# Spreading the indirect gathers of a retrieval layer evenly between the steps of the main work

## The chip, the cores and the metric

The kernel runs on one core of one Trainium2 chip. The metric is device time in microseconds (us) for one execution of the whole program. Lower is better.

## The reference, cut to what matters

One inference step of a one-layer encoder for 1024 prompt rows and 128 sample rows, D = 1024. A mixer (gated convolution, RWKV-7 recurrence, output projection) comes first. A product-key retrieval over 16384 single-neuron experts follows, and it is what the change touches:

```python
sc, pos = lax.top_k(cand, 16)                 # per token and head: the 16 best experts, 8 heads
eidx = jnp.take_along_axis(cidx, pos, axis=-1)
gate = jax.nn.softmax(sc, axis=-1)
u = jnp.take(U, eidx, axis=0)                 # 128 rows of 1024 for every token
act = jax.nn.gelu(jnp.einsum('thkd,td->thk', u, xt))
out = jnp.einsum('thk,thkd->td', gate * act, jnp.take(V, eidx, axis=0))
```

## The kernel before

The 1152 rows are nine tiles ("rows" in the code) of 128 tokens. `base(g)` runs the mixer and the scores for three groups of three tiles: a long middle part (input projections, recurrence), then the merge with `w_pab`, the output projection with `w_o`, and 16 blocks of `peer_wq` with top-16 selections on VectorE. `route` turns the selections of a tile into expert indices and gates.

The retrieval is done in two ways. Four tiles (`DENSE` = 3, 4, 5, 6) go through the whole expert table in `dense()`: a gates stage first, then 128 blocks of experts, each with 24 matmuls of 512 columns in `hidden` and its share of `out_half`, which has 48 such matmuls for half an output of four blocks. The other five tiles gather. A tile needs 128 indirect DMAs from `peer_u`, each of 128 rows of 1024 floats (512 KB), each used by one VectorE multiply with a sum (`dot` in `sparse_u`), and then 128 from `peer_v`, used in groups of four by 8 matmuls that add into PSUM (`summed` in `sparse_v`). These are the u gathers and the v gathers; all go through the queue of GpSimd (POOL) and share the seven buffers `gt` (`NGT`).

`run(main)` places the gathers. The main work is a Python generator, and at each of its `yield`s `run` looks at `P.ns`, a count of the matmul time written so far (162 ns for a float32r matmul of 384 columns, 216 ns for one of 512, and 216 ns for a float32 one of 128). While the side's clock `state[1]` is behind `P.ns`, one more gather is written and the clock goes on by `pace`: outside the dense stage 900 ns where a v tile and a u tile run together, 1500 ns where one runs alone; in the dense stage, what is left of it divided by the gathers left. `split_w` (called for each block of weights) sets a clock that is behind to `P.ns`. `quiet` stops the gathers while `middle` runs its 15 serial steps of inverse on VectorE; what was held up follows at the next `yield` in one go. `side()` takes from the generators in the order 0 0 0 0 0 1 1 1 0 1, where 0 is v and 1 is u, and `sparse_v` has yields that count for no step. The result is: four v gathers, three u gathers, the `summed` of these four v, one u gather. A `dot` is written behind the next u gather; a `summed` comes two gathers after its last row where v is alone.

What is written is not yet the order on an engine. The program is built with a scheduler that goes by its own model of times: an instruction written earlier has precedence, but one that isn't ready there (its buffer not free, its data not landed) is passed by later ones. `behind` ties a `dot` or a `summed` behind the last main instruction of the moment at which it is written. Outside the dense stage, the main matmuls are chained in their written order. On the chip each engine then takes its instructions in the order so fixed.

Of the kernel before, what the change touches and what calls it, by code (L numbers as in the profile page):

```python
# [31 lines left out]
NSL = 25  # L32
LAT = 350
SPREAD = (16, 8)
PACE_B = (900, 1500)
EARLY = 40e3
NGT, NGD = 7, 0
AWAY = [4, 5, 6, 7]
WDMA = 0
QUIET = True  # L40
# [56 lines left out]
def body(ctx, tc, A):  # L97
# [73 lines left out]
                              reason="order of emission")  # L171

    mains = [None, None]
    state = [None, 0.0]
    quiet = [False]

    def mm_ps(shape=(128, 512)):
# [139 lines left out]
    def base(g):  # L317
# [498 lines left out]
        for d in range(KB):  # L816
            if gts[d] is None:
                yield from gates(d)
            back(d)
            if d >= 2:  # L820
                back(d + 1)
            gt = gts[d]
            w = split_w(A["w_pab"][d])
            for q, (yh, yl) in enumerate(((ya_h, ya_l), (yb_h, yb_l))):
                ps = mm_ps()
                proj(ps[:, :n], w, ((lambda k: yh[k]), (lambda k: yl[k])), n, [(4 * q + k, k) for k in range(4)])
                V.scalar_tensor_tensor(gt[q][:, :n], gt[q][:, :n], 1.0, ps[:, :n], op0=OP.add, op1=OP.mult)
            V.tensor_tensor(gt[0][:, :n], gt[0][:, :n], gt[1][:, :n], op=OP.add)
            ms.append(gt[0])
            yield  # L830
# [7 lines left out]
        for hf in range(2):  # L838
            pss = [mm_ps() for _ in tiles]
            for kp in range(4):  # L840
                for kk_, (a, b_) in enumerate(split_w(A["w_o"][hf, kp])):
                    k_ = 2 * kp + kk_
                    mh, ml = split_x(ms[k_][:, :n], "sl", [128, n], NSL)
                    for j, ps in enumerate(pss):
                        ts = slice(j * 128, (j + 1) * 128)
                        P.matmul(ps, mh[:, ts], a, start=k_ == 0, stop=False)
                        P.matmul(ps, mh[:, ts], b_, start=False, stop=False)
                        P.matmul(ps, ml[:, ts], a, start=False, stop=k_ == KB - 1)
                yield
            for j, ps in enumerate(pss):  # L850
                V.tensor_tensor(x2s[j][:, hf * 512:(hf + 1) * 512], ps, x2s[j][:, hf * 512:(hf + 1) * 512], op=OP.add)
        for j, x2 in enumerate(x2s):
# [35 lines left out]
        for hp in range(16):  # L888
            if hp == 8 and not last:
                rows[g + 1] = rows_of(g + 1)  # L890
            ps = mm_ps()
            w = split_w(A["peer_wq"][hp])
            for i, _ in enumerate(proj_steps(ps[:, :n], w, ((lambda k: qh[:, k, :n]), (lambda k: ql[:, k, :n])), n,
                                             full)):
                if i == 3 and hp:
                    top(hp - 1, q)
            q = slot()
            S.activation(q[:, :n], ps[:, :n], AF.Copy)
            yield
# [101 lines left out]
        yield 6 if row == 0 else 2 * SPREAD[until[0] is not None]  # L1001

    more = [None, 0]
    both = [False]

    def gathered():

# [6 lines left out]
    def sparse_u(row, ei, et, gate):  # L1014
        xn = T(sp, [128, D], F32, "xn", 1)
        nc.sync.dma_start(xn, xn2_d[row])
        n2bc = T(sp, [128, D], F32, "gt", NGT)
        nc.sync.dma_start(n2bc, A["norm2_g"].partition_broadcast(128))
        V.tensor_tensor(xn, xn, n2bc, op=OP.mult)
        hu = T(sp, [128, 128], F32, "hu", 3)  # L1020

        def dot(k, ug):
            behind(V.scalar_tensor_tensor(ug, ug, 1.0, xn, op0=OP.mult, op1=OP.mult, accum_out=hu[:, k:k + 1]),
                   mains[0])

        due = None
        for k in range(128):
            ug = gathered()
            G.indirect_dma_start(out=ug, out_offset=None, in_=A["peer_u"],  # L1029
                                 in_offset=bass.IndirectOffsetOnAxis(ap=ei[:, k:k + 1], axis=0))  # L1030
            if due:
                dot(*due)
            due = k, ug
            yield True
        dot(*due)
        sparse_v_q.append((row, hu, et, gate))

    def sparse_v(row, hu, et, gate):
        S.activation(hu, hu, AF.Gelu_apprx_tanh)
        V.tensor_tensor(hu, hu, gate.rearrange("p h k -> p (h k)"), op=OP.mult)  # L1040
        pv = T(psv, [128, D], F32, "sv", 1)
        P.transpose(pv[:, 0:128], hu, ident, side=True)
        ct_ = T(sp, [128, 128], F32, "hu", 3)
        V.tensor_copy(ct_, pv[:, 0:128])

        cw = cex[:, :1024].rearrange("p (two c t w) -> p two c t w", two=2, c=4, w=32)
        c4 = ct_.rearrange("p (c b t) -> p c b t", c=4, t=4)

        def fill(n):
            if n < 8:  # L1050
                V.tensor_copy(cw[:, n % 2, :, :, 31], c4[:, :, n])

        def summed(i, vgs):

            prev = mains[1]
            for hf in range(2):
                for c in (3, 2, 1, 0):
                    lo = 32 * (16 * (i // 4 % 2) + 4 * c + i % 4) + 31 - i
                    q = 32 * c
                    mm = P.matmul(pv[q:q + 32, hf * 512:(hf + 1) * 512], cex[:, lo:lo + 32],  # L1060
                                  vgs[c][:, hf * 512:(hf + 1) * 512], start=i == 0, stop=i == 31, side=True)
                    behind(mm, prev)
                    prev = mm
            if i % 4 == 0:
                fill(i // 4 + 1)

        fill(0)
        due = None
        for i in range(32):
            vgs = []  # L1070
            for c in range(4):
                if c == 2 and due:
                    summed(*due)
                    due = None
                t = 32 * c + i
                vg = gathered()
                G.indirect_dma_start(out=vg, out_offset=None, in_=A["peer_v"],  # L1077
                                     in_offset=bass.IndirectOffsetOnAxis(ap=et[:, t:t + 1], axis=0))
                vgs.append(vg)
                yield True  # L1080
            due = i, vgs
            yield False
            if both[0]:
                summed(*due)
                due = None
                yield False
        if due:
            summed(*due)
        live[0] -= 1
        y = T(sp, [128, D], F32, "gt", NGT)  # L1090
        nc.sync.dma_start(y, x2_d[row])
        for hf in range(2):
            V.tensor_tensor(y[:, hf * 512:(hf + 1) * 512], pv[:, hf * 512:(hf + 1) * 512],
                            y[:, hf * 512:(hf + 1) * 512], op=OP.add)
        finish(row, y, pv)
# [9 lines left out]
    def dense():  # L1105
# [92 lines left out]
        def out_half(eg, hf, ps_):  # L1198
            po = [T(pd, [128, 512], F32, "po", 4) for _ in range(nd)]
            for c in range(EG):  # L1200
# [8 lines left out]
                for j in range(nd):  # L1209
                    ts = slice(j * 128, j * 128 + 128)  # L1210
                    P.matmul(po[j], ph[:, ts], h, start=c == 0, stop=False)
                    P.matmul(po[j], ph[:, ts], lo, start=False, stop=False)
                    P.matmul(po[j], pl[:, ts], h, start=False, stop=c == EG - 1)
            for j in range(nd):
                V.tensor_tensor(acc[:, j, hf * 512:(hf + 1) * 512], po[j], acc[:, j, hf * 512:(hf + 1) * 512],
                                op=OP.add)

        def produced(k):
            g = T(dp, [128, ND], F32, "ge", HLEAD + 2)
            if k in ahead:  # L1220
                nc.sync.dma_start(g, g_d[ahead.index(k)])
            else:
                for _ in hidden(k, g):
                    pass
            return g

        def loaded(eg):
# [1 line left out]
            nc.sync.dma_start(cc, c_d[:, :, :, EG * eg:EG * eg + EG, :].rearrange("j g p a t -> p (j g) a t"))  # L1229
            return cc  # L1230

        gs = [produced(k) for k in range(HLEAD)]
        ccs = [loaded(0)]
        prev = None
        for eg in range(128 // EG):
            cc = ccs.pop(0)
            cur = []
            for c in range(EG):
                k = eg * EG + c
                if k + HLEAD < 128:  # L1240
                    gs.append(produced(k + HLEAD))
                if c == 1 and eg + 1 < 128 // EG:
                    ccs.append(loaded(eg + 1))
                g = gs.pop(0)
# [5 lines left out]
                V.tensor_tensor(pl, g, f32(ph), op=OP.subtract)  # L1250
                cur.append((ph, pl))
                if prev is not None and c % 2 == 1:
                    out_half(eg - 1, c // 2, prev)
                yield
            prev = cur
        for hf in range(2):
            out_half(128 // EG - 1, hf, prev)
            yield
        for j, row in enumerate(DENSE):
            finish(row, acc[:, j])  # L1260
            yield
# [2 lines left out]
    def side():  # L1264

        while True:
# [2 lines left out]
            if two == [None, None]:  # L1269
                return  # L1270
            while two[0] or two[1]:
                for i in (0, 0, 0, 0, 0, 1, 1, 1, 0, 1):
                    both[0] = two[1] is not None
                    if two[i] is None:
                        continue
                    got = next(two[i], None)
                    if got is None:
                        two[i] = None
                    elif got:
                        steps[0] += 1  # L1280
                        yield two.count(None)


# [8 lines left out]
    def run(main):  # L1292

        for _ in main:
            mains[:] = V.last, P.last
            while state[1] < P.ns and not quiet[0]:
                if state[0] is None:
                    if not (sparse_q or sparse_v_q):
                        state[1] = P.ns
# [4 lines left out]
                    state[0] = None  # L1304
                else:
                    state[1] += pace(kind)

    def routes():
        while rest:
# [105 lines left out]
```

## Time and profile before

| | |
|---|---|
| time, median of 3 runs | 3957.97 us (3956.65 to 3962.18) |
| the profiled execution | 3941.97 us, span 3940.2 us |
| mean granted TensorE clock | 0.932 of full speed |
| gathers | 640 of each kind, 671.55 MB of 1065.24 MB moved |

The profile is of one execution. A busy share says how much of a stretch an engine worked; PEclk is the granted TensorE clock, 1.00 being 2.4 GHz and 0.50 being 1.2 GHz. A wait names the engine that stood idle, the tile that it was to write, and what ended the wait.

### The profile page before, as it was taken

The numbers are of one execution on the slowest core, as the hardware profiler recorded it, in microseconds if no ns is written. First come the engines' busy times: TensorE is split into PE (matmuls) and PEld (weight loads), VectorE is DVE, ScalarE is ACT, GpSimd is POOL, SyncE is SP. The second block draws the span as 40 slices with busy tenths as digits, with TensorE's granted clock in tenths as the row PEclk, the third lists the DMA queues.
The fourth block names the chain that finished last, engine by engine and source line by source line (L and its number), as shares of the span: only waits on it lengthen the run. The fifth ranks groups of instructions, "written<-read, shape, count | busy, mean of one in ns | idle before, by whom it ended". The sixth has DMA issues, their size and how long they took to land. (4 is left out here: it accounts for less than half of the span.)

```text
span 3940.2 us, 56486 instructions
## 1 busy us (share of the span) xinstructions
PE 3416.1 (87%) x18870; PEld 2633.5 (67%) x18870; DVE 2769.8 (70%) x7554; ACT 1486.2 (38%) x3511; POOL 1644.5 (42%) x1553
## 2 busy tenths in 40 slices
PE   7999977878877786887767999699999999999998
PEld 6778876656665564555555777477777777776676
DVE  4655799887788777758688865499976666664344
ACT  5454533344332332332325877522232222232222
POOL 1000004444455565555555555455544444443331
PEclk9999988878988897888888999899999999999999
DMA  3212527666898888788998989999999989998884
GB/s 101 76 59 88 167 87 258 207 200 196 309 340 302 312 296 300 275 299 309 336 322 296 333 323 337 344 329 362 338 333 330 327 311 330 322 318 294 296 291 161
DMA packets 434019, 1065.24 MB, mean 270 GB/s; under 512 B 47040, under 2 KB 127040, under 8 KB 431680
## 3 DMA queue, kind: packets, MB, share of 16 engines
q0 software_dynamic: 184464, 671.55, 48.0%
q1 hardware_dynamic: 201312, 271.04, 20.8%
q10 hardware_dynamic: 47952, 119.03, 8.2%
q8 instruction: 150, 2.46, 0.2%
q14 instruction: 141, 1.16, 0.1%
HBM read 1000.55 MB, written 61.28 MB: 269 GB/s over the span
## 5 line engine op out<-in xcount | busy, mean ns | idle before, releaser
L1029 POOL DMA_INDIRECT gt<-peer_u,ei x640 | 764.5, 1194 | 1160.4 <-DVE gt L159 442.5
L159 DVE SCALAR_TENSOR_TENSOR gt<-gt,xn 128x1024 f32<-128x1024 f32 x640 | 770.2, 1220 | 230.6 <-DMA gt<-peer_u,ei 212.5
L1077 POOL DMA_INDIRECT gt<-peer_v,et x640 | 713.3, 1115 | 484.1 <-PE sv L142 283.4
L142 PE MATMUL mm<-xT,wh 128*128 128x384 f32 (+1 forms) x2880 | 891.7, 368 | 21.4 <-ACT wh L246 21.2
L142 PE MATMUL po<-vh,ph 128*128 128x512 f32 x2048 | 651.7, 392 | 8.1 <-ACT vh L1205 7.8
L142 PEld LDWEIGHTS mm<-xT,wh 128*128 128x128 f32 x2880 | 561.7, 200 | 88.3 <-issue 41.4
L142 PE MATMUL mm<-xT,wl 128*128 128x384 f32 (+1 forms) x1440 | 513.6, 357 | 57.5 <-DVE wl L159 56.0
L142 PE MATMUL sv<-gt,c 128*32 128x512 f32 x2560 | 338.1, 650 | 146.4 <-DMA gt<-peer_v,et 142.2
L142 PEld LDWEIGHTS po<-vh,ph 128*128 128x128 f32 x2048 | 385.0, 188 | 105.3 <-ACT vh L1205 10.3
L142 PE MATMUL ph<-xth,uh 128*128 128x512 f32 x1024 | 412.5, 403 | 16.5 <-ACT ge L1178 11.0
L246 ACT ACTIVATE wh<-raw 128x512 fp32r<-128x512 f32 x432 | 269.8, 629 | 385.5 <-PE mm L142 193.6
L142 PE MATMUL ph<-xth,ul 128*128 128x512 f32 x1024 | 407.6, 398 | 3.6 <-DVE ul L159 3.4
L142 PE MATMUL po<-vl,ph 128*128 128x512 f32 x1024 | 402.1, 393 | 9.5 <-DVE vl L159 9.2
L142 PE MATMUL ph<-xtl,uh 128*128 128x512 f32 x1024 | 402.1, 393 | 1.8 <-DVE xtl L159 1.8
L159 DVE TENSOR_TENSOR wl<-raw,wh 128x512 fp32r<-128x512 f32 x432 | 294.7, 685 | 118.9 <-ACT wh L246 116.8
L142 PEld LDWEIGHTS mm<-xT,wl 128*128 128x128 f32 x1440 | 288.0, 200 | 81.8 <-DVE wl L159 71.2
L142 PEld LDWEIGHTS sv<-gt,c 128*32 128x32 f32 x2560 | 70.5, 115 | 307.4 <-DMA gt<-peer_v,et 162.2
L1205 ACT ACTIVATE vh<-vr 128x512 fp32r<-128x512 f32 x256 | 158.2, 626 | 268.3 <-PE po L142 165.9
L142 PEld LDWEIGHTS ph<-xth,uh 128*128 128x128 f32 x1024 | 193.8, 189 | 97.6 <-issue 34.4
L1178 ACT ACTIVATE ge<-ph 128x512 f32<-128x512 f32 x128 | 76.3, 596 | 479.8 <-PE ph L142 439.4
L142 PEld LDWEIGHTS po<-vl,ph 128*128 128x128 f32 x1024 | 192.9, 188 | 55.7 <-DVE vl L159 15.4
L142 PEld LDWEIGHTS ph<-xth,ul 128*128 128x128 f32 x1024 | 193.4, 189 | 54.1 <-issue 6.7
(247 smaller groups left out, 5223.0 us busy)
## 6 DMA issues: line engine op xcount, KB each, us to landing
ur<-u_t SPq DMA_DIRECT2D x256, 256.0 KB, 6.4
vr<-peer_v ACTq DMA_DIRECT2D x256, 256.0 KB, 6.2
raw<-w_in SPq DMA_DIRECT2D x240, 256.0 KB, 3.5
c<-ct ACTq DMA_DIRECT2D x16, 2048.0 KB, 10.3
cc<-c SPq DMA_DIRECT2D x32, 1024.0 KB, 16.8
raw<-peer_wq SPq DMA_DIRECT2D x96, 256.0 KB, 5.1
raw<-w_pab SPq DMA_DIRECT2D x48, 256.0 KB, 5.4
raw<-w_o SPq DMA_DIRECT2D x48, 256.0 KB, 5.2
```

The lines of the kernel that those rows point to most:

```text
L142: ins = nc.tensor.matmul(out, lhsT, rhs, **kw)
L159: self.last = getattr(nc.vector, name)(*a, **kw)
L246: S.activation(h, part, AF.Copy)
L1029: G.indirect_dma_start(out=ug, out_offset=None, in_=A["peer_u"], in_offset=bass.IndirectOffsetOnAxis(ap=ei[:, k:k + 1], axis=0))
L1077: G.indirect_dma_start(out=vg, out_offset=None, in_=A["peer_v"], in_offset=bass.IndirectOffsetOnAxis(ap=et[:, t:t + 1], axis=0))
L1178: S.activation(g, ps, AF.Gelu_apprx_tanh)
L1205: S.activation(h, raw, AF.Copy)
```

## The change

- `PACE_B` goes from (900, 1500) to (750, 1300) ns.
- Between two gathers there is at least half a pace of `P.ns` (`GAP`, `state[2]`), so that a `yield` of the main work gives one gather at most.
- The main work gets more `yield`s: in the `w_pab` merge, in the output projection, in the `peer_wq` blocks, in `hidden` where `produced` calls it, and in `out_half`.
- The order becomes four v gathers, four u gathers. Uses go into a list `later`, and each is written once three more gathers of either kind have been written (`USE_U`, `USE_V`). At the end of a tile what is left is written at once.

```diff
-PACE_B = (900, 1500)
+PACE_B = (750, 1300)
+USE_U, USE_V = 3, 3
+GAP = 0.5
...
-                proj(ps[:, :n], w, ((lambda k: yh[k]), (lambda k: yl[k])), n, [(4 * q + k, k) for k in range(4)])
+                yield from proj_steps(ps[:, :n], w, ((lambda k: yh[k]), (lambda k: yl[k])), n,
+                                      [(4 * q + k, k) for k in range(4)])
...
                         P.matmul(ps, ml[:, ts], a, start=False, stop=k_ == KB - 1)
-                yield
+                        yield
...
                 if i == 3 and hp:
                     top(hp - 1, q)
+                yield
...
-    both = [False]
+
+    later = []
+
+    def use(kind=None):
+
+        for e in list(later):
+            if (e[0] <= steps[0]) if kind is None else (e[1] == kind):
+                later.remove(e)
+                e[2](*e[3])
...
-            if due:
-                dot(*due)
-            due = k, ug
+            later.append((steps[0] + 1 + USE_U, 1, dot, (k, ug)))
             yield True
-        dot(*due)
+        use(1)
...
+                if c == 3:
+                    later.append((steps[0] + 1 + USE_V, 0, summed, (i, vgs)))
                 yield True
-            due = i, vgs
-            yield False
-            if both[0]:
-                summed(*due)
-                due = None
-                yield False
-        if due:
-            summed(*due)
+        use(0)
...
                     P.matmul(po[j], pl[:, ts], h, start=False, stop=c == EG - 1)
+                    if j % 2 == 1:
+                        yield
...
-                for _ in hidden(k, g):
-                    pass
+                yield from hidden(k, g)
...
-                for i in (0, 0, 0, 0, 0, 1, 1, 1, 0, 1):
-                    both[0] = two[1] is not None
+                for i in (0, 0, 0, 0, 1, 1, 1, 1):
                     if two[i] is None:
                         continue
-                    got = next(two[i], None)
-                    if got is None:
+                    if next(two[i], None) is None:
                         two[i] = None
-                    elif got:
+                    else:
                         steps[0] += 1
+                        use()
                         yield two.count(None)
...
-            while state[1] < P.ns and not quiet[0]:
+            while state[1] < P.ns and state[2] <= P.ns and not quiet[0]:
...
                     state[1] += pace(kind)
+                    state[2] = P.ns + GAP * pace(kind)
```

The callers of `produced` and `out_half` become `yield from` in the same way.

## Rows read from the trace of the kernel before

**Rows 1.** The page's first part: busy time, share of the span, instructions.
```profile
span 3940.2 us, 56486 instructions
PE 3416.1 (87%) x18870; PEld 2633.5 (67%) x18870; DVE 2769.8 (70%) x7554; ACT 1486.2 (38%) x3511; POOL 1644.5 (42%) x1553
```

**Rows 2.** Busy time by stretch: length, then each engine; granted clock, DMA share, GB/s.
```profile
0.00:600.00 600.00, 524.92 (x3222) 454.28 (x3223) 398.88 (x1427) 288.08 (x751) 40.81 (x84) 0.95 0.32 100
600.00:985.00 385.00, 305.10 (x1919) 245.85 (x1919) 321.44 (x928) 150.47 (x467) 160.63 (x147) 0.84 0.65 213
985.00:1500.00 515.00, 410.18 (x2310) 317.44 (x2309) 414.68 (x1305) 172.20 (x381) 277.36 (x241) 0.90 0.88 312
1500.00:2085.00 585.00, 420.47 (x2638) 299.20 (x2636) 425.43 (x1367) 171.57 (x465) 319.33 (x283) 0.83 0.86 306
...
2500.00:2860.00 360.00, 305.60 (x1344) 238.47 (x1344) 296.81 (x521) 105.55 (x198) 188.43 (x156) 0.95 0.97 346
2860.00:3540.00 680.00, 673.30 (x3192) 510.02 (x3194) 456.19 (x755) 198.65 (x345) 306.69 (x262) 1.00 0.92 325
```

**Rows 3.** Waits of the whole span: us in total, times, longest us.
```profile
POOL gt L1029 <- PE sv L142: 395.7, 61, 17.9
...
DVE gt L159 <- DMA gt<-peer_u,ei: 212.5, 113, 10.2
```

**Rows 4.** Waits of TensorE, 985 to 2085 us.
```profile
PE sv L142 <- DMA gt<-peer_v,et: 101.3, 25, 14.3
```

**Rows 5.** The timeline of GpSimd: start us, us, instruction, [idle before <-releaser].
```profile
1650.96 0.98 POOL L1029 DMA_INDIRECT gt<-peer_u,ei  x1 [3.72 <-PE sv L142]
...
1655.97 0.94 POOL L1077 DMA_INDIRECT gt<-peer_v,et  x1 [0.30 <-issue]
...
1659.70 0.93 POOL L1029 DMA_INDIRECT gt<-peer_u,ei  x1 [0.30 <-issue]
1666.43 1.74 POOL L1029 DMA_INDIRECT gt<-peer_u,ei  x1 [5.80 <-PE sv L142]
```

**Rows 6.** DMA issues: count, median us from issue to landing.
```profile
gt<-peer_u,ei POOLq DMA_INDIRECT x640, 7.3
gt<-peer_v,et POOLq DMA_INDIRECT x640, 7.0
```

**Rows 7.** Busy time by stretch, of line 1077 (v gathers) alone.
```profile
985.00:1930.00 945.00, 248.54 (x208) 0.87 0.86 307
1927.00:2047.00 120.00, 36.68 (x28) 0.95 0.89 313
```

**Rows 8.** The same of line 1029 (u gathers).
```profile
583.00:985.00 402.00, 156.87 (x123) 0.84 0.66 216
985.00:1930.00 945.00, 239.77 (x212) 0.87 0.86 307
1927.00:2047.00 120.00, 32.33 (x29) 0.95 0.89 313
```

**Rows 9.** The page's costliest groups: count, busy us, mean ns, idle before.
```profile
L159 DVE SCALAR_TENSOR_TENSOR gt<-gt,xn 128x1024 f32<-128x1024 f32 x640 | 770.2, 1220 | 230.6 <-DMA gt<-peer_u,ei 212.5
...
L142 PE MATMUL sv<-gt,c 128*32 128x512 f32 x2560 | 338.1, 650 | 146.4 <-DMA gt<-peer_v,et 142.2
```

**Rows 10.** The timeline of TensorE, 1514 to 1534 us.
```profile
1514.81 3.64 PE L142 MATMUL sv<-gt,c 128*32 128x512 f32 x16 [10.06 <-DMA gt<-peer_v,et]
1530.60 3.35 PE L142 MATMUL sv<-gt,c 128*32 128x512 f32 x16 [12.15 <-DMA gt<-peer_v,et]
```

**Rows 11.** Two inversions' stretches, tile bc alone: DVE, ACT, granted clock, DMA.
```profile
1482.00:1541.00 59.00, 7.37 (x57) 0.00 (x0) 0.68 0.82 287
1610.00:1628.00 18.00, 6.76 (x57) 0.00 (x0) 0.84 0.93 337
```

**Rows 12.** Waits of TensorE, 2500 to 2860 us.
```profile
PE po L142 <- DVE vl L159: 8.9, 7, 2.0
PE po L142 <- ACT vh L1205: 7.8, 6, 2.6
```

More of the change, by code (lines that the diff above doesn't have):

```diff
@@ L173, in body @@
     mains = [None, None]
-    state = [None, 0.0]
+    state = [None, 0.0, 0.0]
     quiet = [False]
@@ L1067, in sparse_v @@
         fill(0)
-        due = None
         for i in range(32):
@@ L1071, in sparse_v @@
             for c in range(4):
-                if c == 2 and due:
-                    summed(*due)
-                    due = None
                 t = 32 * c + i
@@ L1079, in sparse_v @@
                 vgs.append(vg)
+                if c == 3:
+                    later.append((steps[0] + 1 + USE_V, 0, summed, (i, vgs)))
                 yield True
-            due = i, vgs
-            yield False
-            if both[0]:
-                summed(*due)
-                due = None
-                yield False
-        if due:
-            summed(*due)
+        use(0)
         live[0] -= 1
@@ L1230, in loaded @@
             return cc
-        gs = [produced(k) for k in range(HLEAD)]
+        gs = []
+        for k in range(HLEAD):
+            gs.append((yield from produced(k)))
         ccs = [loaded(0)]
@@ L1240, in dense @@
                 if k + HLEAD < 128:
-                    gs.append(produced(k + HLEAD))
+                    gs.append((yield from produced(k + HLEAD)))
                 if c == 1 and eg + 1 < 128 // EG:
@@ L1252, in dense @@
                 if prev is not None and c % 2 == 1:
-                    out_half(eg - 1, c // 2, prev)
+                    yield from out_half(eg - 1, c // 2, prev)
                 yield
@@ L1256, in dense @@
         for hf in range(2):
-            out_half(128 // EG - 1, hf, prev)
-            yield
+            yield from out_half(128 // EG - 1, hf, prev)
         for j, row in enumerate(DENSE):
```

## The prediction

> **What bounds the kernel now.** I read the page's first part, then the stretches, then the waits, and last the timelines of GpSimd and TensorE inside the stretches that lose time. On the whole span TensorE is the busiest engine, 87%, and VectorE has 70% [rows 1]. The stretches say where the 13% lie. From 2860 us on, the dense loop keeps TensorE at 673.3 of 680 us at full clock, so there only TensorE work can be saved. In the first 600 us, which have hardly a gather, it has 524.9 of 600 us at a granted clock of 0.95. In the three stretches from 600 to 2085 us, in which gathers run beside the mixer of the second and third group, it is idle for 1485 - 305.1 - 410.2 - 420.5 = 349 us, and the granted clock is 0.83 to 0.90 [rows 2]. What the change can win lies mostly there.
>
> The waits name two owners: GpSimd, whose u gathers wait 395.7 us for the `summed` matmuls, and VectorE, whose `dot`s wait 212.5 us for rows to land [rows 3]. TensorE waits 101.3 us for v rows between 985 and 2085 us [rows 4]. The timeline of GpSimd shows why. From 1650.96 us it issues eight gathers back to back, stands idle for 5.80 us until `summed` is done, and starts the next eight at 1666.43 us [rows 5]. This is a closed loop: with seven buffers, the fourth u gather needs the buffer of the first v row, so it needs `summed`, which needs the last v row. That row was issued at 1655.97 us; 7.0 us from issue to landing [rows 6] and about 3.4 us of `summed` [rows 10] give 1666.4 us, which is where the next eight begin. So eight gathers cannot take less than about 15.5 us, 1.9 us each.
>
> Is the loop what sets the rate, or the pace? From 985 to 1930 us 208 + 212 = 420 gathers run in 945 us, 2.25 us each; in the `peer_wq` part of the third group 28 + 29 = 57 run in 120 us, 2.11 us each [rows 7, 8]. By the code, that part writes 16 x (24 x 162 + 3 x 216) ns = 72.6 us of `P.ns`, which at 900 ns is 81 gathers. Only 57 were executed there. The writing has run ahead of what the loop can deliver, so here a gather's place comes from its buffer and not from the pace. With u alone it is otherwise: 123 gathers in 402 us, 3.27 us each [rows 8], far slower than any loop.
>
> **The change part by part.**
>
> *Pace with u alone, 1500 to 1300 ns.* The stretch of 402 us shrinks in main work by 2/15, so the first tile's u gathers end up to 54 us sooner. VectorE is already 321 of 385 us busy there [rows 2], so I take three quarters, 40 us. The loop then delivers 40 / 2.11 = 19 gathers more before the dense stage, which then has 19 fewer v gathers of the third tile. One v gather is 338.1 / 640 = 0.53 us of TensorE [rows 9], in the dense stage nothing hides it, and before it TensorE has idle time for it: -10 us. Ends: 0 and -13 us.
>
> *Pace with both, 900 to 750 ns.* By the last paragraph the loop sets the rate: 0. If the pace were obeyed, the 476 gathers from 985 to 2047 us [rows 7, 8] would be 476 x 900 / 750 = 571, 95 more, -50 us by the same price.
>
> The Trainium skill, page "DMA: Bandwidth & Descriptors", section "Anatomy of one DMA — SWDGE (gpsimd) path", fits a transfer issued by GpSimd as 2.0 us plus its bytes over 436e3 bytes per us. For 512 KB that makes an estimate of 3.2 us, under half of what this trace shows, and the loop would have slack for the faster pace: by it the term would be -50 us and not 0. The trace's 7.0 us stand, with the DMA engines 86 to 93% busy.
>
> *No bursts (`GAP`).* A stop of `quiet` is followed by a lump of gathers with their uses at one place. At 1514.81 and 1530.60 us TensorE does two `summed` with nothing between them and idles 10.06 and 12.15 us before them [rows 10]. With half a pace between gathers there would be main work between. I take half of these 22.2 us, -11; the ends are 0, if the buffers keep the lumps, and the whole 101.3 us [rows 4].
>
> *Uses three gathers later.* For a `dot` it was one. Behind a waiting `dot` VectorE's main work stands, the `wl` halves among it, and TensorE behind these. If it all came right, the part of the 212.5 us in which TensorE idles too, 349 / 1485 of it, would come back, -50 us. But the later place only holds where the writing isn't ahead of the loop, and the waits lie where it is: 0. A `summed` stood four paces of 900 ns behind its last v row and now stands three of 750 ns, 2.25 against 3.6 us. Over the 64 groups of two tiles 1.35 us each could cost 86 us; I take 0, since the loop and not the written place decides when it can run.
>
> *More yields in the dense stage.* They write no instruction, so their own cost is 0. Gathers no longer come in lumps of about five behind 48 matmuls. Where u runs alone, 2500 to 2860 us, VectorE has 297 of 360 us and TensorE waits 8.9 + 7.8 us for the halves of the value table [rows 12]; I take half, -8. After 2860 us there is next to nothing to win [rows 2].
>
> Sum: -10 - 11 - 8 = -29 us. The profiled execution took 3942 us (span 3940), so it would take 3913; the median of the runs lies 16 us above it, and the same step from 3958 gives 3929 us. I hold 8 us, 0.2%, for what a measurement of this kernel can tell from no change.
>
> **The rivals.**
>
> *The pace is obeyed* (faster by more). For it: with u alone no loop binds; the loop's floor of 15.5 us is below the 18 us per eight that were seen [rows 5, 7, 8], so some cycles wait for TensorE's order and not for DMA. Against it: 57 gathers where 81 were written. 95 + 19 gathers leave the dense stage, 114 x 0.53 = 60 us, and with -11 and -8 that is -79: 3879 us. This is also where the page's 3.2 us would lead.
>
> *The backlog stretches the inversions* (slower). If the loop can't deliver faster, a faster pace only lengthens what is written and not yet done, and older side work has precedence over the serial VectorE steps that `quiet` is meant to protect. In the third group three of the four inversions take 18 to 21 us, one takes 59 us for the same 57 instructions [rows 11], with TensorE clocked down to 0.68. Each further one that is stretched so costs 59 - 18 = 41 us. With one, and nothing won by `GAP`, it is -18 + 41 = +23, 3981 us; with two +64, 4022 us. It decides from the first one on. Against it: the loop itself admits only one group of eight per 15.5 us, so most inversions meet no more than that.
>
> *It does nothing.* If buffers place the gathers everywhere outside the dense stage, and TensorE is full inside it, all terms are within 8 us of 0: 3950 to 3966 us.
>
> **How the numbers follow.** Forecast 0.40, own range 3905 to 3948 us. Pace obeyed 0.18. Stretched inversions 0.26. Nothing 0.16. The prediction is 3929 us. Faster is the first two, 0.58; same 0.16; slower 0.26. The range goes down past the second case's 3879 us to 3860, for its distance can be larger if `GAP` wins more than half, and up to 4000 us, which holds the third case with one stretched inversion. Outside lie about 0.04 below and 0.12 above.
>
> **What would show it.** Right: the cycle of eight stays at 15 to 17 us; the first v gather comes some 40 us earlier; the dense stage begins with about 19 gathers fewer left; the two idle times of 10 to 12 us before adjacent `summed` are gone; TensorE's waits for v rows from 985 us to the dense stage fall well below 101 us. Wrong: the cycle falls under 15 us or the dense stage begins with over 60 gathers fewer (the pace binds); an inversion of the third group other than the second takes over 40 us (backlog); VectorE crowds out the dense loop where u runs alone, because the backlog of `dot`s is served before the splits; or the stretch with u alone gets slower, since its `dot`s are denser on a VectorE that is nearly full.

## The result and the profile after

The changed kernel takes 4053.43 us (median of 4 runs, 4050.43 to 4064.04), the kernel before 3957.68 us beside it: a ratio of 1.0244 (95% interval 1.0224 to 1.0265). It is 2.4% slower; 3929 us and a range up to 4000 us were forecast. The profiled execution has a span of 4062.2 us, 122.0 us more than before. Of these, some 26 us are spread between executions: the one profiled before lies 16 us under its median (3942 and 3958 us), the one profiled after 11 us over its own (4064 and 4053 us).

The page's first part shows that TensorE has the same instructions, and only 23 us more of busy time. So some 99 of the 122 us are idle time.

```profile
span 4062.2 us, 56634 instructions
PE 3439.5 (85%) x18870; PEld 2648.8 (65%) x18870; DVE 2774.8 (68%) x7554; ACT 1490.5 (37%) x3513; POOL 1627.8 (40%) x1553
```

The stretches say where (same columns and bounds as [rows 2], and the one from 2085 us).

```profile
600.00:985.00 385.00, 301.89 (x1901) 243.52 (x1899) 327.54 (x937) 145.12 (x454) 163.72 (x154) 0.85 0.68 220
985.00:1500.00 515.00, 393.76 (x2090) 301.36 (x2091) 388.16 (x1205) 161.60 (x348) 281.26 (x240) 0.87 0.87 309
1500.00:2085.00 585.00, 372.24 (x2394) 243.04 (x2392) 362.17 (x936) 134.30 (x394) 319.13 (x287) 0.79 0.83 293
2085.00:2500.00 415.00, 356.05 (x2157) 267.09 (x2158) 292.70 (x1204) 226.66 (x525) 198.72 (x215) 0.91 0.86 307
...
2860.00:3540.00 680.00, 672.14 (x3145) 513.04 (x3144) 444.98 (x739) 192.26 (x335) 258.26 (x242) 1.00 0.90 307
```

Up to 985 us little differs. From 985 to 1500 us TensorE does 220 matmuls fewer, at a granted clock of 0.87 and not 0.90; from 1500 to 2085 us 244 fewer, at 0.79 and not 0.83, with 48 us less busy time. GpSimd's busy time in these two stretches is within 4 us of what it was, and so is the DMA share, within 0.03. From 2860 us on TensorE is as full as before. So the loss lies where the change was to win, beside the mixer, and there the same gathers go with less main work.

The waits of the whole span answer to [rows 3]. The first line is of the kernel before, the others are of the changed one (its line 1040 is the u gather, 1082 the v gather, 161 a VectorE instruction, 144 a matmul):

```profile
POOL gt L1029 <- DVE gt L159: 442.5, 133, 21.0
```

```profile
POOL gt L1040 <- DVE gt L161: 557.1, 135, 19.4
DVE gt L161 <- DMA gt<-peer_u,ei: 356.3, 140, 9.7
POOL gt L1082 <- PE sv L144: 327.0, 69, 8.3
...
POOL gt L1040 <- PE sv L144: 258.1, 47, 9.5
...
PE sv L144 <- DMA gt<-peer_v,et: 206.7, 38, 12.2
```

The u gathers' waits for `summed` have fallen from 395.7 to 258.1 us, those of the v gathers have grown from 283.4 to 327.0. VectorE's `dot`s wait more for their rows, 356.3 and not 212.5 us, and the u gathers wait 557.1 us for these `dot`s, and not 442.5. From 985 to 2085 us alone, TensorE's waits for v rows, which were to fall well below the 101.3 us of [rows 4], are

```profile
PE sv L144 <- DMA gt<-peer_v,et: 175.2, 32, 12.2
```

The loop itself is as it was. GpSimd's timeline, at the place of [rows 5], has the next eight gathers begin 16.5 us after the first eight (1651.31 to 1667.78), again after a wait for `summed`:

```profile
1651.31 1.31 POOL L1040 DMA_INDIRECT gt<-peer_u,ei  x1 [4.70 <-PE sv L144]
...
1658.55 0.94 POOL L1082 DMA_INDIRECT gt<-peer_v,et  x1 [0.30 <-DVE bc L161]
...
1667.78 1.90 POOL L1040 DMA_INDIRECT gt<-peer_u,ei  x1 [3.69 <-PE sv L144]
```

The median landing is now 6.3 us for either kind. The Trainium skill's fit ("DMA: Bandwidth & Descriptors", section "Anatomy of one DMA — SWDGE (gpsimd) path"), which gave an estimate of 3.2 us for these bytes, still doesn't hold here; the trace's number is twice that.

Two u tiles and two v tiles, 512 gathers, are issued from 987 to 2111 us, 2.2 us each; before it was 1005 to 2144, 2.2 us too. What has moved is the main work beside them. The inversions of the third group are no longer than in [rows 11] (same view, second and third):

```profile
1531.00:1589.00 58.00, 7.47 (x57) 0.00 (x0) 0.67 0.85 306
1657.00:1678.00 21.00, 7.04 (x58) 0.00 (x0) 0.82 0.93 328
```

But the fourth begins at 1726.6 us with 462 gathers issued, where it began at 1676.5 us with 430. Behind the third group's output projection comes the costliest place. ScalarE has one wait of 155.2 us, and its timeline shows which instruction stood there:

```profile
ACT sv L237 <- DVE gt L161: 155.2, 1, 155.2
```

```profile
2115.84 0.60 ACT L237 ACTIVATE sv<-gt 128x512 f32<-128x512 f32 x1 [155.24 <-DVE gt L161]
2116.38 0.19 ACT L237 ACTIVATION_READ_ACCUMULATOR sv<-gt 128x1 f32 x1
2116.47 0.58 ACT L237 ACTIVATE rk<-scr 128x512 f32<-128x512 f32 x1
```

Line 237 is the Square in `rstd_of`. The first one (`sv<-gt`) belongs to `finish`, the step that ends a gathered tile, here the second one; the one behind it (`rk<-scr`) is the main work's own, for the norm ahead of `peer_wq`. Both take their small tile from the tag "rstd", and in the order of this program the one of `finish` comes first. It needs all `summed` of its tile, and ten groups of these are still to come, nothing between them. The main work's Square, next in ScalarE's order, starts only behind it, at 2116.47 us; from here on this is called the block. TensorE's timeline (three of the ten) and the stretch:

```profile
1984.35 3.60 PE L144 MATMUL sv<-gt,c 128*32 128x512 f32 x16 [12.25 <-DMA gt<-peer_v,et]
1999.54 3.64 PE L144 MATMUL sv<-gt,c 128*32 128x512 f32 x16 [11.59 <-DMA gt<-peer_v,et]
...
2107.70 3.36 PE L144 MATMUL sv<-gt,c 128*32 128x512 f32 x16 [11.44 <-DMA gt<-peer_v,et]
```

```profile
1971.00:2117.00 146.00, 32.99 (x152) 5.44 (x144) 49.31 (x81) 1.16 (x4) 79.23 (x77) 0.57 0.79 276
```

Each of the nine in this stretch waits 11 to 12 us for its rows. In 146 us TensorE works 33 us, at a mean granted clock of 0.57, near the lower of its two levels (1.2 of 2.4 GHz). While ScalarE waits, 79 gathers are issued, one in 2.0 us. The kernel before has no three `summed` groups in a row in its order.

At the first Gelu of the dense stage (the start of its table load) the account stands so, before and after, u first and then v (columns: stretch, length, GpSimd busy and gathers, clock, DMA share, GB/s):

```profile
583.00:2105.00 1522.00, 440.42 (x375) 0.86 0.81 284
583.00:2105.00 1522.00, 298.72 (x248) 0.86 0.81 284
```

```profile
583.00:2286.00 1703.00, 442.64 (x384) 0.83 0.81 281
583.00:2286.00 1703.00, 376.16 (x323) 0.83 0.81 281
```

384 + 323 = 707 gathers are done and the Gelu comes at 2286 us; before it was 375 + 248 = 623 and 2105 us. That is 84 gathers more and 181 us more, 2.15 us for each. The rest, from the Gelu to the end, is 1776 us and not 1835: 59 us less, 0.70 us for each gather not left over. 181 - 59 = 122 us, the whole difference of the spans. The 2.15 us are a mean over two unlike parts: the block's 155 us, and on balance 26 us for all that comes ahead of it and behind it.

### The profile page after: what moved, and what is told of

It reads as the page before. It is cut to its first block, busy times and chain, and to the rows that moved or that the text cites. A ratio compares the mean times of both kernels' runs of the same rounds, so it can differ in the third digit from the quotient of the medians.

```text
span 4062.2 us, 56634 instructions
## 1 busy us (share of the span) xinstructions
PE 3439.5 (85%) x18870; PEld 2648.8 (65%) x18870; DVE 2774.8 (68%) x7554; ACT 1490.5 (37%) x3513; POOL 1627.8 (40%) x1553
## 4 chain that ended last, share of the span: by engine, by line
PE 55%; DVE 15%; DMA 15%; issue 8%; POOL 4%; ACT 3%; DVEq 0%; POOLq 0%; SPq 0%; ACTq 0%
PE po L144 15%; PE mm L144 14%; PE ph L144 12%; PE sv L144 7%; DMA gt<-peer_u,ei 5%; DMA gt<-peer_v,et 5%; PE rk L144 5%; DVE gt L161 4%; POOL gt L1082 2%; DVE wl L161 2%; DVE o L161 2%; POOL gt L1040 2%; DVE sl L161 1%; PE rk L149 1%; DMA ur<-u_t 1%
## 5 line engine op out<-in xcount | busy, mean ns | idle before, releaser
L1040 POOL DMA_INDIRECT gt<-peer_u,ei x640 | 733.8, 1147 | 1123.1 <-DVE gt L161 557.1
L161 DVE SCALAR_TENSOR_TENSOR gt<-gt,xn 128x1024 f32<-128x1024 f32 x640 | 776.6, 1222 | 383.8 <-DMA gt<-peer_u,ei 356.3
L1082 POOL DMA_INDIRECT gt<-peer_v,et x640 | 707.0, 1105 | 649.0 <-PE sv L144 327.0
L144 PE MATMUL sv<-gt,c 128*32 128x512 f32 x2560 | 354.8, 678 | 206.7 <-DMA gt<-peer_v,et 206.7
L161 DVE TENSOR_TENSOR ul<-ur,uh 128x512 fp32r<-128x512 f32 x256 | 170.7, 688 | 108.0 <-ACT uh L1168 106.8
L161 DVE TENSOR_TENSOR vl<-vr,vh 128x512 fp32r<-128x512 f32 x256 | 175.8, 689 | 77.4 <-ACT vh L1205 77.1
```

Of the source, the lines that this page charges most:

```text
L144: ins = nc.tensor.matmul(out, lhsT, rhs, **kw)
L161: self.last = getattr(nc.vector, name)(*a, **kw)
```

## The experiments

All runs in one table. "Written" counts the gathers that the program's order has ahead of the dense stage, "done" those issued by its first Gelu in the trace, and "rest" is the span less the time of that Gelu. Each ratio is to the kernel before measured beside the run. Beside e1 to e4 it took 3950 us, beside the later runs 3979 to 3993 us, so times in us are compared within the upper or the lower part of the table only; c0 is the kernel before, traced again beside the later runs. One kernel measured twice differs by 0.2 to 0.3% in its ratio (e1 and e18, e16 and e19).

| run | what it is | written | done | first Gelu, us | rest, us | ratio (95% interval) |
|---|---|---|---|---|---|---|
| before | | 645 | 623 | 2105 | 1835 | 1 |
| after | | 700 | 707 | 2286 | 1776 | 1.0244 (1.0224 to 1.0265) |
| e1 | after, own buffer | 700 | 658 | 2157 | 1860 | 1.0169 (1.0150 to 1.0189) |
| e2 | before, own buffer | 645 | 623 | 2124 | 1848 | 0.9997 (0.9984 to 1.0010) |
| e3 | before, new pace | 724 | 723 | 2280 | 1795 | 1.0335 (1.0305 to 1.0365) |
| e4 | after, old pace | 614 | 615 | 2109 | 1845 | 1.0007 (0.9985 to 1.0029) |
| c0 | before, traced again | 645 | 623 | 2145 | 1842 | 1 |
| e7 | before, new pace for both kinds only | 695 | 702 | 2328 | 1788 | 1.0355 (1.0316 to 1.0394) |
| e11 | before, new pace for u alone only | 665 | 654 | 2199 | 1823 | 1.0104 (1.0073 to 1.0135) |
| e8 | e3, own buffer | 724 | 667 | 2200 | 1838 | 1.0099 (1.0060 to 1.0138) |
| e9 | before, pace (1000, 1600) | 584 | 591 | 2094 | 1883 | 0.9964 (0.9940 to 0.9987) |
| e5 | before, pace (1100, 1700) | 531 | 539 | 2070 | 1917 | 1.0005 (0.9986 to 1.0025) |
| e10 | after, pace (1000, 1500) | 547 | 559 | 2112 | 1903 | 1.0028 (1.0006 to 1.0049) |
| e13 | before, half rows | 645 | 651 | 2124 | 1778 | 0.9835 (0.9806 to 0.9864) |
| e14 | after, half rows | 700 | 707 | 2196 | 1764 | 0.9915 (0.9886 to 0.9944) |
| e15 | e8, at most 645 written | 645 | 651 | 2182 | 1837 | 1.0076 (1.0048 to 1.0103) |
| e16 | e1, at most 645 written | 645 | 651 | 2190 | 1811 | 1.0029 (1.0007 to 1.0052) |
| e17 | e8, at most 584 written | 584 | 595 | 2136 | 1882 | 1.0070 (1.0048 to 1.0093) |
| e18 | e1 again | 700 | 658 | 2190 | 1860 | 1.0136 (1.0113 to 1.0158) |
| e19 | e16 again | 645 | 651 | 2191 | 1804 | 1.0047 (1.0026 to 1.0068) |

**The pace, the rest, and the block (e1 to e4).** The edit for e1 and e2, in `rstd_of`, gives `finish` of a gathered tile a tag of its own, so that its Square no longer comes before the main rows':

```diff
-        ss = T(sp, [128, 3], F32, "rstd", 4)
+        ss = T(sp, [128, 3], F32, "rstd" if ps is None else "rstf", 4 if ps is None else 2)
```

e3 and e4 change one line each way:

```diff
-PACE_B = (900, 1500)
+PACE_B = (750, 1300)
```

Expected of e1, e2, e3 and e4:

> Theory A (the block): in the changed kernel the sum of squares that ends the second gathered tile and those of the third group's main rows share four small buffers, which are given out in written order. The gathered tile is written ahead and done late, so the main rows wait behind ten groups of summed. With a buffer of its own for the gathered tiles the block of 155 us goes and some 100 to 130 us come back: 3920 to 3960 us. Theory B (supply): each gather that is pushed before the dense stage costs its share of a 15.5 us cycle wherever it stands, so the buffer changes little: 4030 to 4060 us.

> The same buffer in the kernel before, where no such block is seen. Both theories: 3950 to 3966 us, no change. If it were clearly faster, the buffer would be worth something by itself, and the gain of the buffer in the changed kernel would not all be the block's.

> Only the pace of the change, in the kernel before. Theory A: the pace alone brings the second tile's end before the main rows' sums: a block of about eight cycles, +80 to +110 us, 4035 to 4070 us. Theory B: the pace pushes the gathers, so 4030 to 4060 as well. Theory C (the later uses and the shorter distance of summed do the harm): 3950 to 3970 us.

> The changed kernel with the old pace (900, 1500). Theory A: no block, 3920 to 3965 us. Theory B: the same. Theory C: 4020 us or more.

The pace alone does all the harm, 3.3%, more than either theory had (4079 us against 4070 at most); all the other edits together do nothing at the old pace, and win back 0.9% at the new one (1.0244 against 1.0335). The buffer alone changes nothing in the kernel before. In the changed kernel it removes the block, whose wait of 155.2 us falls to 18.2 us at most, and brings the first Gelu 129 us sooner, but only 0.75% of the time comes back (1.1% by e18, the same kernel measured again), between the two theories. The block is one cost, and not the only one. The longer waits of the u gathers for the `dot`s are not where the loss lies: in e3, with the old uses, they are 444.1 us, and e3 is the slower kernel.

Beside e2, e1 has its first Gelu 33 us later, with 35 gathers more done, and from there to the end it is 12 us longer, although 35 gathers fewer are left. A place where the second part is lost stands in e1's waits of TensorE, and in its stretches, where the gates stage passes into the dense loop:

```profile
PE ph L144 <- ACT ge L1178: 42.4, 1, 42.4
```

```profile
2550.00:2600.00 50.00, 24.85 (x106) 20.71 (x106) 43.27 (x110) 27.11 (x62) 44.24 (x37) 0.62 0.87 300
2600.00:2650.00 50.00, 17.94 (x68) 14.64 (x69) 28.01 (x46) 9.19 (x16) 14.33 (x12) 0.63 0.92 317
```

TensorE works 43 of these 100 us, at a granted clock of 0.62 to 0.63, while VectorE is busy for 43 of 50 us in the first half; the longest such wait in e2 is 17.6 us.

**Which half of the pace (e7, e11), the block's price at the pace alone (e8), and a slower pace (e9).** e7 has PACE_B (750, 1500), e11 (900, 1300), e9 (1000, 1600); e8 is e3 with the buffer's edit.

> The kernel before with PACE_B (750, 1500): only the half of the pace that holds while both kinds of gather run. Theory B (each gather written ahead of the dense stage beyond what the loop delivers costs about 2.2 us of loop there and saves about 0.7 us in the dense stage): this half carries the harm, first Gelu of the dense stage about 150 us later with some 80 more gathers done, 4050 to 4100 us. Theory C (the harm comes from the u half, denser dots where VectorE is 83% busy): 3945 to 3970 us. The order of this kernel has 14 adjacent summed groups ahead of the third group's main rows; at the loop's 15.5 us each they would be up to 217 us of waiting in one place.

> The kernel before with PACE_B (900, 1300): only the half of the pace that holds while u gathers run alone. Theory B: no backlog from the loop before both kinds run, u gathers of the first tile end 20 to 40 us sooner, the dense stage begins at nearly the same time: 3935 to 3970 us (the forecast's own term for this half was -10 us). Theory C: this half carries the harm, 4020 us and more, with u gathers 1 to 128 not sooner or VectorE's share of the stretch over 95%.

> The kernel before with PACE_B (750, 1300) and a buffer of its own for the rstd of a gathered tile's finish. It measures what the block of summed groups behind a shared buffer costs where the pace is the only change. If the price of the block is only partly real, as in the changed kernel (164 us at its place, 36 us at the end): 4020 to 4060 us. If the block is what the pace costs: 3950 to 3975 us. If nothing: 4070 to 4090 us.

> The kernel before with PACE_B (1000, 1600). Theory B as a slope (fewer gathers ahead of the dense stage are worth 1.2 to 1.5 us each at any pace, and some 20 fewer would be done there): 3915 to 3935 us. Rival (the kernel before stands at the balance: less backlog saves nothing more there, and the gathers left over cost 0.5 to 0.7 us each in the dense stage or trail behind its end): 3955 to 3985 us. Either way the peer_wq part of the third group and the first Gelu of the dense stage come sooner than in the kernel before.

The half for both kinds carries the harm, 3.6% (by this ratio 4090 us beside a kernel before of 3950 us, within theory B's range), with a block of its own. From 985 to 1927 us nothing tells e7 from c0, neither in main work nor in gathers (c0 first):

```profile
985.00:1927.00 942.00, 722.82 (x4226) 529.53 (x4225) 689.70 (x2040) 289.15 (x730) 487.20 (x431) 0.85 0.83 293
```

```profile
985.00:1927.00 942.00, 719.49 (x4238) 528.38 (x4237) 689.82 (x2042) 288.57 (x728) 486.52 (x433) 0.86 0.84 295
```

Then ScalarE waits 218.7 us for `finish`, and 109 gathers are issued meanwhile, one in 2.0 us. So the faster pace neither speeds the gathers nor harms the main work up to there; it writes 14 `summed` groups and the `finish` behind them ahead of the main work's norm. Here is ScalarE's wait in e7, then in e3 and in e8:

```profile
ACT sv L235 <- DVE gt L159: 218.7, 1, 218.7
```

```profile
ACT sv L235 <- DVE gt L159: 129.8, 2, 128.2
```

```profile
ACT sv L235 <- DVE gt L159: 13.9, 2, 12.4
```

In e8 the buffer takes 2.4% back (1.0335 to 1.0099), two to three times what it does in the changed kernel. 1% is left (3989 us by the ratio, beside 3950), between the first two of the three cases expected, and as much as e11 has with the faster pace for u alone and no block.

e11 is the run that speaks on the forecast's own term. It costs 1.0% (3991 us by the ratio, beside 3950), which lies between what the two theories had. No block is in its order: no more than two `summed` groups stand in a row. The stretches from 985 us to the first Gelu, of c0 and of e11:

```profile
985.00:2145.00 1160.00, 877.01 (x5054) 646.91 (x5056) 863.10 (x2729) 358.59 (x885) 606.85 (x539) 0.85 0.85 300
```

```profile
985.00:2199.00 1214.00, 910.25 (x5189) 668.84 (x5189) 873.10 (x2746) 367.19 (x916) 629.76 (x562) 0.84 0.83 295
```

The 128th u gather comes at 968 us and not at 1010: 42 us sooner. But the first Gelu comes 54 us later, with 31 gathers more done (654 against 623), and TensorE is idle 304 us in the stretch and not 283. Its rest is 19 us shorter, 0.62 us for each of the 31.

Where the 54 us arise can be followed on the main work's weight splits on VectorE (tile `wl`). From the 205th to the 301st of them, c0 and then e11 take

```profile
759.00:1213.00 454.00, 370.83 (x2209) 289.43 (x2208) 356.69 (x1059) 173.84 (x476) 199.45 (x185) 0.87 0.75 254
```

```profile
756.00:1242.00 486.00, 381.62 (x2271) 293.74 (x2270) 371.77 (x1096) 173.57 (x474) 228.98 (x210) 0.86 0.76 264
```

The same splits take 32 us longer with 25 more gathers beside them, 1.3 us for each, which is less than the loop's 2.2 us and near the 1.22 us that a `dot` holds VectorE [rows 9]. VectorE is busy for 15 us more, and TensorE idle for 21 us more. Whether VectorE's `dot`s set this price was not tried.

e9, the other way, gains 0.4%. It has 32 gathers fewer done, its first Gelu comes 51 us sooner than in c0 and its rest is 41 us longer. By the ratio that is 3936 us beside 3950: a gain just short of what theory B's slope gives, and more than the rival's balance. The price of a gather is not the same on both sides of the kernel before.

**The far side, and halved gathers (e5, e10, e13, e14).** e5 has PACE_B (1100, 1700), e10 is the changed kernel with (1000, 1500). e13 and e14 gather half of each row (the other half of the gathered products is left out), with the counts of matmuls and the `dot`'s columns kept:

```diff
+    def half_rows(t):
+        return t.rearrange("r (a c) -> (r a) c", a=2)
...
-            G.indirect_dma_start(out=ug, out_offset=None, in_=A["peer_u"],
+            G.indirect_dma_start(out=ug[:, :512], out_offset=None, in_=half_rows(A["peer_u"]),
```

> The kernel before with PACE_B (1100, 1700), the other side of the balance. Theory B with a kink (below about 590 gathers ahead of the dense stage the loop no longer holds the main work up, so each gather left over only costs its 0.5 to 0.9 us there, and the order has a tail of six summed groups behind the last dense matmul): 3965 to 4010 us, with the first Gelu of the dense stage no more than 20 us sooner than at (1000, 1600). If the gain goes on with the slope of the fast side, 1.3 us a gather: 3900 to 3930 us.

> The changed kernel with PACE_B (1000, 1500). Theory B: as with the kernel before at (1000, 1600), some 20 to 30 gathers fewer ahead of the dense stage, 3935 to 3960 us on a chip where the kernel before takes 3950 to 3958. If the rest of the change wins at a slow pace what it won at the fast one (0.9%): 3905 to 3930 us.

> The kernel before, but each gather brings only the first 512 of the 1024 columns of its rows, as 2 KB runs (the dot is done in two halves on these columns and summed reads them twice, so VectorE and TensorE have about the same work; the sparse rows of the output are not those of the reference). Theory B (a closed loop, landing plus use, prices a gather ahead of the dense stage): landing falls from 7 us towards 4.5 us, eight gathers take 12 to 13 us in place of 15.5 us, and the kernel takes 3830 to 3900 us. If the loop is not set by landing: 3930 to 3970 us.

> The changed kernel with the same halved gathers. Theory B: with the loop quick enough for the faster pace, the extra gathers ahead of the dense stage are nearly free, and the changed kernel is no longer slower than its counterpart: within 0.7% of the kernel before with halved gathers. Theory D (the harm lies in the written order itself, with VectorE and GpSimd, whatever a row's landing takes): it stays 2% or more above it.

e5 ends where the kernel before does, between the two cases expected: 75 us sooner at the first Gelu (24 us sooner than e9, where at most 20 were expected), 75 us longer behind it. The changed kernel at a slow pace is no better than the kernel before, so the 0.9% that its other edits win at the fast pace is not to be had at a slow one. With halved rows the gap between the two kernels falls from 2.4% to 0.9915 / 0.9835 = 1.0081, two thirds of it gone, a little short of the 0.7% expected. Beside the kernel before, e13 gains 1.65%, 65 us, the slow end of theory B's range. Two things are mixed in e14: the loop is quicker (512 gathers in 1069 us for e13, 1170 in c0), and the halved kernel's order has no block (at most three `summed` groups in a row). The halving itself gave less than expected: the loop went from 2.3 to 2.1 us a gather, not to 1.6.

**Number or density (c0, e15 to e19).** A cap on what is written ahead of the dense stage, at the same pace:

```diff
+CAP = 645
...
-            while state[1] < P.ns and not quiet[0]:
+            while state[1] < P.ns and not quiet[0] and (until[0] is not None or steps[0] < CAP):
```

> The kernel before itself, for a trace on the chip of these runs, where it takes 1% longer than on the first chip: all milestones up to the first gathers within 1% of the first trace, and the extra 1% in the stages with gathers.

> The kernel before with PACE_B (750, 1300) and the buffer of its own (ratio 1.0099 without a cap), and no more than 645 gathers written ahead of the dense stage: as many as the kernel before writes, in place of 724. Theory B (the number of gathers ahead of the dense stage is what costs, 1.3 us each net): ratio 0.998 to 1.004. Theory D (their density does the harm: dots and summed packed closer beside the main work): ratio 1.008 and more.

> The changed kernel with the buffer of its own (ratio 1.0169 without a cap) and at most 645 gathers written ahead of the dense stage in place of 700. Theory B: 0.996 to 1.005. Theory D: 1.012 and more.

> As e15 with at most 584 gathers ahead of the dense stage, the number that the kernel before writes at PACE_B (1000, 1600), whose ratio was 0.9964. Theory B: 0.992 to 0.999. Theory D: 1.005 and more. If the gathers left over hurt in the dense stage: 1.000 to 1.005.

> The changed kernel with the buffer of its own, once more, beside the capped one on one chip. If the cap is what took 1.0169 to 1.0029: 1.013 to 1.019 here as well. If the two chips differ by it: 1.002 to 1.008.

> The same with at most 645 gathers written ahead of the dense stage, once more. If the cap does it: 1.000 to 1.006 and at least 1% below the run without it. If the chips differ by it: within 0.4% of the run without it.

c0 is as expected: its first gather comes at 589 us and not 583, and most of the longer time lies behind it.

e18 and e19 were measured side by side. The cap takes 1.0136 to 1.0047, 0.9%, with intervals well apart, just short of the 1% expected (e1 and e16, measured apart: 1.0169 to 1.0029). Their first Gelu comes at the same time, 2190 and 2191 us, with 658 and 651 gathers done. So the 55 gathers fewer were not work done sooner, but backlog: written ahead of the dense stage and served inside it. The stretch from the 31st to the 40th Gelu, of e18 and then of e19:

```profile
2487.00:2694.00 207.00, 137.60 (x676) 111.62 (x675) 151.82 (x368) 111.82 (x260) 126.63 (x113) 0.74 0.90 316
```

```profile
2476.00:2658.00 182.00, 124.60 (x692) 99.78 (x691) 121.97 (x318) 106.50 (x259) 85.66 (x90) 0.82 0.83 295
```

Nearly the same number of matmuls takes 207 and 182 us; e18 has 70 gathers there and e19 47. By the 56th Gelu (2944 and 2883 us) e18 is 61 us behind, with 269 gathers since the first Gelu against 242: 27 more, 2.3 us for each.

In the kernel before at the new pace the cap gives nothing sure (1.0099 to 1.0076, with intervals that overlap), and e17 with its 584 written is 1.1% above e9 with 584. From the first Gelu on the two are alike (1882 and 1883 us); what differs is how densely the gathers lie ahead of it: by the start of the third group's fourth inversion e17 has done 478 gathers and e9 414, and which comes at 1754 us in the one and at 1671 us in the other, 1.3 us for each of the 64. So theory B, for which only the number counts, holds for the changed kernel within its expected range (e16, e19); in the kernel before, where the gathers lie counts too.

## Why the prediction was wrong

**The step that failed** is one premise in the two terms on the pace, that gathers done or written sooner cost nothing ahead of the dense stage: "before it TensorE has idle time for it" for u alone, and "the loop sets the rate: 0" for both. The dense side was sized well where the gathers were done sooner: 0.53 us a gather was forecast; the rest shrank by 0.70 us a gather in the changed kernel, 0.62 in e11, 0.68 in e7. The other side was set to nothing and is the larger one. For each gather more, the first Gelu came 2.15 us later in the changed kernel, 1.7 in e11 (54 / 31), 2.3 in e7 (183 / 79). TensorE has the idle time, but not the order for it. Where main work stands behind a row of `summed` groups, it waits until the loop has brought their rows, 2.0 us a gather in both blocks. Where it doesn't, the price is lower and not nothing: 1.3 us a gather in the stretch of e11 shown above, 33 us for 35 gathers from e2 to e1.

**Pace with u alone, -10 us: +1.0% in e11.** Its mechanism came as described: the last u gather of the first tile 42 us sooner (40 forecast), 31 gathers fewer left (19 forecast), 19 us shorter from the first Gelu on. 54 us went ahead of it. In the changed kernel the first v gather is 18 us sooner.

**Pace with both, 0: +3.6% in e7.** "By the last paragraph the loop sets the rate: 0" is right in its first half. In the changed kernel the rate stayed at 2.2 us a gather, and the cycle at 16.5 us; e7 did the same work as c0 up to 1927 us. That the time therefore stays was the error: where the loop can't follow, a faster pace sets more undelivered gathers ahead of the main work in the order, and e7 paid for them in one wait of 218.7 us. The forecast held the sign that told it, 57 gathers done where 81 were written, as a reason for no effect.

**`GAP`, -11; uses later, 0; yields, -8.** e4 has all of these at the old pace and measures +0.07% (-0.15 to +0.29), against -19 us, 0.5%. Together they are nothing there; which of them wins the 0.9% at the new pace was not tried apart. e4 also has 31 gathers fewer written ahead of the dense stage than the kernel before. At the new pace the two idle times of [rows 10] are gone from their place, but ten others stand in a row. The later `dot`, held to be worth nothing, came with more waiting of GpSimd for VectorE, 557.1 us against 442.5, and e3, without it, is slower all the same.

**The rivals.** "The pace is obeyed" got its place right, 84 gathers fewer in the dense stage against 114, and its sign wrong, by the same free gather. "The backlog stretches the inversions" got the sign and the agent, written work that isn't done and has precedence, but not the place: no inversion of the third group but the second took over 24 us in the changed kernel. The cost sat in three others: spread over the stretch to the fourth inversion (with 32 gathers more, +50 us against the trace before and +20 us against c0), in the block ahead of `peer_wq` (155 us of ScalarE's wait), and, where the block was taken away, at the entry to the dense loop (61 us in e18 against e19). Of the signs listed for "wrong", "over 60 gathers fewer" came true, read there as the pace that binds; VectorE's crowding at the dense loop was named too.

**What stays open.** In the changed kernel the block is worth 0.75 to 1.1% and the cap 0.9%; of the 2.4% some 0.3 to 0.5% are left (e16, e19). In the kernel before, the faster pace for u alone costs 1.0% (e11), and 0.7% are left without a block and with a cap (e15, e17). By the start of the third group's fourth inversion these traces show main work put off by 0.8 to 1.0 us against c0 for each gather that is done sooner, but no single wait that holds it. How much of the narrowing in e14 is the quicker loop and how much the missing block was not separated.

The version that beats both, by little, is e9, the kernel before with both paces slowed by 100 ns: 0.9964 (0.9940 to 0.9987).

## What to carry to other kernels

Before you move work into an engine's idle time, ask what the engine is idle for. Where it waits for the loop that the moved work comes from, and main work stands behind that wait, each piece cost the loop's period here (2.0 us a gather) and not its own length (0.53 us of TensorE). When what is written ahead exceeds what a closed loop delivers, a faster schedule gives no more of it but a longer queue, and the queue has precedence over what stands behind it. Look in the order for tiles that main and side work share by tag: a shared small buffer can put an instruction of the side work, with everything it needs, ahead of the main work.

## What the runs showed that was not expected

- Halving each gather's bytes cut the traffic of the mixer stretch from 300 to 196 GB/s and the DMA share from 0.85 to 0.64, but the loop's time per gather only from 2.3 to 2.1 us (e13 against c0). Bytes are the lesser part of what sets this loop.
- The faster pace for both kinds changed neither the gathers nor the main work for 942 us (e7 and c0 up to 1927 us), and then cost its 3.6% in one wait.
- A shared tag of four [128, 3] tiles held ScalarE for 128 to 219 us (e3, the changed kernel, e7), and whether it did so hung on the pace alone: the order before has no such block, and a buffer of its own there is worth nothing (e2).
